# RWKV scan of a two-block network: two heads as full-array products, gram products of the heads in turn

## The chip, the cores and the metric

The kernel runs on one core of a Trainium2 chip. The metric is the device time of one execution in microseconds (us), the median of several runs. The engines are TensorE (PE in the rows, its weight loads PEld), VectorE (DVE), ScalarE (ACT), GpSimd (POOL) and SyncE (SP, which issues the DMAs here).

## What is computed

Two network blocks run one after the other on 256 latent and 256 context tokens of width 2048. The first holds sliding-window attention and latent attention, the second a mixer of pooling and RWKV-7 heads, and then an attention layer. The change lies in the RWKV part alone: 16 heads of width 64, two directions, and for each head a state of 64x64 that is updated token by token over 512 tokens:

```
def step(S, xs):
    r, w, k, v, a, b = xs
    sa = jnp.einsum('bhvk,bhk->bhv', S, a)
    S = S * w[:, :, None, :] + sa[..., None] * b[:, :, None, :] + v[..., None] * k[:, :, None, :]
    return S, jnp.einsum('bhvk,bhk->bhv', S, r)
```

The decay w and the gate a come out of low-rank products (`tanh(shift(wd)) @ w2`, `shift(ad) @ a2`), and the result of the scan is normalised over each head of each token.

## The kernel before

The scan is done in chunks: NCH = 8 chunks of L = 64 tokens. One unit of work, the generator `rwkv(b, d)`, takes two heads (block b of 128 feature rows, head 0 on partitions 0 to 63, head 1 on 64 to 127) and one direction d; there are 16 units. A unit makes the decays (L1156 to L1191), the scaled keys BK and queries AQ (L1197 to L1214), a bonus product `bon` (L1220), the gram products of keys and queries of each chunk (L1241) with masked evictions (L1244 to L1246), the transposed keys BKs (L1265) and values SV (L1274, L1279), and the inverse of a triangular matrix of each chunk (from 8 rows upwards, L1341 to L1366), which leaves TT.

Then comes the chain over the 8 chunks, one step for each. In a step five pairs of fp32 products, one product for each head, all write into one PSUM bank named `chain`: AQ's first part times SV (L1376), which VectorE copies to Rp (L1378); AQ's second part times SV (L1380); TT times Rp (L1388), copied into SV by VectorE and ScalarE (L1389, L1390); BKs times SV (L1393; not in the last step), added to the decayed state by VectorE (L1399, one instruction for each head); and QB times SV (L1404), which ScalarE evicts to y with its row sums (L1405). The next step starts from the state that L1399 wrote. The rows name a matmul's part of the array: 128\*64 and 64\*64 for the products of the chain, of which the two heads use two different column halves, 64\*128 for the gram products, 128\*128 for the whole array. An fp32 product leaves two records in the trace, a fp32r product one.

The units do not run alone. The loop over weight slices (`weights`, L327 on; products by `mm3`, L352 to L354) calls `fill` after each slice, and that moves every active unit on by one `yield`; up to four units are active, 12 yields apart. So TensorE's queue holds products `a` of the dense layers (fp32r, 128x512, three for each tile, with operands split into whi and wlo by L323 on ScalarE and L324 on VectorE) and among them the units' small products. The order of each engine's queue is fixed when the program is built, by a scheduler that lays out the instructions by the time that it takes them to need; at run time each engine goes through its queue in order and waits where an operand is not there.

Of the kernel before, what the change touches and what calls it, by code (L numbers as in the profile page):

```python
# [18 lines left out]
P = 128  # L19
# [4 lines left out]
L = 64  # L24
# [92 lines left out]
class Net:  # L117
# [933 lines left out]
    def ev_consts(self, ph):  # L1051
        nc, I = self.nc, self.I
        def load(n, shape):
            t = ph.tile(shape, F32, name="c_" + n)
            nc.sync.dma_start(out=t, in_=I[n])
            return t
        self.bones = load("bones", [P, P])
        self.bsel = load("bsel", [P, 2])
        self.smask = ph.tile([P, NT], F32, name="smask")
        nc.gpsimd.memset(self.smask, 1.0)  # L1060
        nc.gpsimd.memset(self.smask[:, 0:NT:L], 0.0)
        self.gmask = load("gmask", [P, P])
# [8 lines left out]
        nc.vector.tensor_scalar(self.kai, self.v("k_a", 0, 8), -0.5, 1.0, ALU.mult, ALU.add)  # L1071
        self.xscr = [self.pD.tile([1, BLK], F32, name=f"xscr{j}") for j in range(2)]
# [64 lines left out]

    def rwkv(self, ph, b, d, pads, lora, yscr, sums):
# [54 lines left out]
        AQ = ph.tile([P, 2, NCH, P], F32, tag="AQ", name=self.nm("AQ"), bufs=2)  # L1193
        BK = ph.tile([P, NCH, 2, L], F32, tag="BK", name=self.nm("BK"), bufs=BKB)
        for hh in range(2):
            r_ = half[hh]
            nc.vector.scalar_tensor_tensor(AQ[r_, hh, :, 0:L], ch(kkn)[r_], -1.0, Dp[r_, :, 0:L], ALU.mult, ALU.mult)  # L1197
# [14 lines left out]
        for hh in range(2):  # L1212
            r_ = half[hh]
            nc.vector.tensor_tensor(AQ[r_, hh, :, L:], ch(r)[r_], Dp[r_, :, 1:], op=ALU.mult)  # L1214
# [16 lines left out]

        NTr = ph.tile([P, NCH, L], F32, tag="NT", name=self.nm("NT"), bufs=NTB)
        QB = ph.tile([P, NCH, L], F32, tag="QB", name=self.nm("QB"), bufs=2)
        for hh in range(2):
            r_, o_ = half[hh], half[1 - hh]
            for c4 in range(0, NCH, 4):
                cs = slice(c4, c4 + 4)
                pb = self.bank("gram")
                for c in range(c4, c4 + 4):
                    lhs = BK[r_, c, :, :].rearrange("p a t -> p (a t)")  # L1240
                    mm(pb[:, (c - c4) * P : (c - c4 + 1) * P], lhs, AQ[r_, hh, c, :], start=True, stop=True)  # L1241
                pv = pb.rearrange("p (c t) -> p c t", c=4)
                mk = self.gmask.unsqueeze(1).broadcast_to([P, 4, P])
                nc.vector.tensor_tensor(NTr[r_, cs, :], pv[r_, :, 0:L], mk[r_, :, 0:L], op=ALU.mult)  # L1244
                nc.vector.tensor_tensor(QB[r_, cs, :], pv[r_, :, L:], mk[r_, :, L:], op=ALU.mult)
                nc.vector.tensor_tensor(AQ[o_, hh, cs, :], pv[o_], mk[o_], op=ALU.mult)  # L1246
            yield
# [11 lines left out]
        BKs = ph.tile([P, 2, NCH, L], F32, tag="BKs", name=self.nm("BKs"), bufs=2)  # L1259
        for hh in range(2):  # L1260
            r_ = half[hh]
            pb = self.bank("bkt")
            for c in range(NCH):
                src = BK[r_, c, :, :].rearrange("p a t -> p (a t)")
                nc.tensor.transpose(pb[:, c * L : (c + 1) * L], src, self.ident[r_, r_])  # L1265
            nc.scalar.copy(BKs[:, hh], ch(pb))
        yield
        SV = ph.tile([P, 2, NCH + 1, L], F32, tag="SV", name=self.nm("SV"), bufs=2)

        for c0 in (0, 1):  # L1270
            pb = self.bank("vt")
            for n in range(4 - c0):
                s = slice((2 * n + c0) * L, (2 * n + c0 + 2) * L)
                nc.tensor.transpose(pb[:, n * P : (n + 1) * P], v[:, s], self.ident)  # L1274
            if c0:
                for hh, c in ((1, NCH - 1), (0, 0)):
                    r_, o_ = half[hh], half[1 - hh]
                    o = 3 * P + hh * L
                    mm(pb[o_, o : o + L], v[r_, c * L : (c + 1) * L], self.ident[r_, r_], start=True, stop=True)  # L1279
# [34 lines left out]
        X2 = ph.tile([64, 16, 16], F32, tag="X2", name=self.nm("X2"))  # L1314
# [19 lines left out]
        TT = ph.tile([P, NCH, L], F32, tag="TT", name=self.nm("TT"), bufs=TTB)  # L1334
# [22 lines left out]
        nc.vector.tensor_tensor(TT, pairs(Z1, TT16), TT16, op=ALU.add)  # L1357
        yield
        pb = self.bank("x2")
        for c in range(NCH):  # L1360
            for q in (0, 64):
                mm(pb[q : q + 32, c * 32 : c * 32 + 32], Z2[q + 32 : q + 64, c, :], TT[q + 32 : q + 64, c, 32:64],
                   start=True, stop=True, tile_position=(q + 32, q))
        pv = pb[:, 0:256].rearrange("p (c t) -> p c t", c=NCH)
        nc.vector.tensor_copy(TT[0:32, :, 32:64], pv[0:32])
        nc.scalar.copy(TT[64:96, :, 32:64], pv[64:96])  # L1366

        y = ph.tile([P, NCH + 1, L], F32, tag="y", name=self.nm("y"), bufs=1)
# [3 lines left out]
        ps = self.bank("chain")  # L1372
        for c in range(NCH):
            last = c == NCH - 1
            for hh in range(2):
                mm(ps[half[hh], 0:64], AQ[:, hh, c, 0:L], SV[:, hh, c, :], start=True, stop=True)  # L1376
            Rp = ph.tile([P, L], F32, tag="Rp", name=self.nm("Rp"), bufs=2)
# [8 lines left out]
            for hh in range(2):  # L1386
                r_ = half[hh]
                mm(ps[r_, 64:128], TT[r_, c, :], Rp[r_], start=False, stop=True, skip_group_check=True)  # L1388
            nc.vector.tensor_copy(SV[half[0], 0, c, :], ps[half[0], 64:128])  # L1389
            nc.scalar.copy(SV[half[1], 1, c, :], ps[half[1], 64:128])  # L1390
            if not last:
                for hh in range(2):
                    mm(  # L1393
                        ps[half[hh], 128:192], BKs[:, hh, c, :], SV[:, hh, c, :],
                        start=False, stop=True, skip_group_check=True,
                    )
                for hh in range(2):
                    r_ = half[hh]
                    nc.vector.scalar_tensor_tensor(  # L1399
                        SV[r_, hh, c + 1, :], ps[r_, 128:192], DL[r_, c : c + 1], SD[r_], ALU.mult, ALU.add  # L1400
                    )
# [6 lines left out]
        y8 = y[:, 0:NCH]  # L1408
        wide = lambda t: t.unsqueeze(2).broadcast_to([P, NCH, L])
        nc.vector.tensor_scalar(mean, mean, 1.0 / L, None, ALU.mult)  # L1410
        nc.vector.tensor_tensor(y8, y8, wide(mean), op=ALU.subtract)
        sq = self.t512("sq").rearrange("p (c t) -> p c t", c=NCH)
        nc.scalar.activation(sq, y8, AF.Square)
# [6 lines left out]
        nc.vector.tensor_tensor(y8, y8, wide(rs), op=ALU.mult)  # L1420
        nc.scalar.copy(y[:, NCH], y[:, 0])
# [4 lines left out]
        for c0 in (0, 1):  # L1426
            pb = self.bank("yt")
            for n in range(4):
                src = y[:, 2 * n + c0 : 2 * n + c0 + 2, :].rearrange("p c t -> p (c t)")
# [570 lines left out]
```

## Time and profile before

| what | value |
|---|---|
| median of 3 runs | 3386.61 us (3378.92 to 3392.72) |
| profiled execution | 3385.91 us, span 3384.1 us |
| TensorE busy | 3198.0 us (95%), 21218 instructions |
| VectorE busy | 2051.4 us (61%) |
| ScalarE busy | 1541.6 us (46%) |
| GpSimd busy | 195.8 us (6%) |
| RWKV stretch | 1620 to 2640 us of the span |

A matmul's record lasts longer than TensorE is held by it, since matmuls are pipelined: what one costs is read from the time from its start to the start of the next one. "Busy" of TensorE can so be near 100% while the starts lie far apart.

### The profile page before, as it was taken

The page shows a single profiled execution, that of the slowest core. Times are in us where ns is not written, and L with a number is a line of the kernel's source. Part 1 is how long each engine was busy: PE and PEld are TensorE (multiplying, and loading weights), DVE is VectorE, ACT ScalarE, POOL GpSimd, SP SyncE. Part 2 cuts the span into 40 slices and gives each one's busy share as a digit, 9 for nine tenths or more (in the row PEclk, how much of TensorE's full clock was granted, in tenths as well). Part 3 has the DMA queues.
Part 4 walks back from the last instruction along what each step waited for, and adds up shares of the span by engine and source line. Part 5 has one row for each costly group of instructions (what it writes and reads, how often), then busy time and mean ns, then how long its engine had stood idle before and what let it go on. Part 6 is the DMA issues. An engine that isn't in the chain of part 4 may idle for free. (4 is left out here: it accounts for less than half of the span.)

```text
span 3384.1 us, 56050 instructions
## 1 busy us (share of the span) xinstructions
PE 3198.0 (95%) x21218; PEld 2384.4 (70%) x21218; DVE 2051.4 (61%) x4487; ACT 1541.6 (46%) x3461; POOL 195.8 (6%) x277
## 2 busy tenths in 40 slices
PE   5999999989989999898999989999999999899998
PEld 2567777767877777665766666666666678778887
DVE  2456455543476666442776676777777655867767
ACT  2424444442366655442344434444444433636654
POOL 0000000000001110000000000000000001200000
PEclk8999999999999999999999999999999999999999
DMA  7843444358654655988534222222323444544454
GB/s 299 307 161 126 144 140 144 131 198 292 213 166 155 212 193 194 369 340 320 170 119 125 76 76 79 73 73 66 99 80 93 133 168 131 174 129 144 132 174 157
DMA packets 270784, 556.27 MB, mean 164 GB/s; under 512 B 122928, under 2 KB 150704, under 8 KB 244912
## 3 DMA queue, kind: packets, MB, share of 16 engines
q1 hardware_dynamic: 270512, 552.68, 49.0%
q8 instruction: 167, 2.74, 0.3%
q14 instruction: 105, 0.86, 0.1%
HBM read 517.46 MB, written 35.13 MB: 163 GB/s over the span
## 5 line engine op out<-in xcount | busy, mean ns | idle before, releaser
L324 DVE TENSOR_TENSOR wlo<-raw,whi 128x512 fp32r<-128x512 f32 (+2 forms) x1000 | 658.7, 668 | 610.4 <-ACT whi L323 573.3
L352 PE MATMUL a<-hhi,whi 128*128 128x512 f32 (+1 forms) x2752 | 975.9, 357 | 32.6 <-ACT whi L323 29.6
L323 ACT CAST whi<-raw 128x512 fp32r<-128x512 f32 (+2 forms) x1000 | 591.8, 599 | 865.1 <-PE a L353 448.9
L353 PE MATMUL a<-hlo,whi 128*128 128x512 f32 (+1 forms) x2752 | 950.5, 347 | 0.2 <-DVE hlo L445 0.2
L354 PE MATMUL a<-hhi,wlo 128*128 128x512 f32 (+1 forms) x2752 | 938.6, 349 | 5.6 <-DVE wlo L324 5.1
L352 PEld LDWEIGHTS a<-hhi,whi 128*128 128x128 f32 x2752 | 524.3, 191 | 192.9 <-ACT whi L323 79.6
L354 PEld LDWEIGHTS a<-hhi,wlo 128*128 128x128 f32 x2752 | 518.5, 191 | 72.5 <-DVE wlo L324 14.1
L353 PEld LDWEIGHTS a<-hlo,whi 128*128 128x128 f32 x2752 | 525.3, 191 | 54.2 <-issue 3.0
L352 PE MATMUL a<-whi,hhi 128*128 128x512 f32 (+1 forms) x672 | 262.8, 401 | 16.1 <-ACT sq L613 5.9
L353 PE MATMUL a<-wlo,hhi 128*128 128x512 f32 (+1 forms) x672 | 264.5, 394 | 0.3
L456 POOL TENSOR_TENSOR rs<-st,mhalf 128x4 f32<-128x4 f32 (+3 forms) x109 | 140.9, 1293 | 2097.5 <-DVE st L453 1910.8
L354 PE MATMUL a<-whi,hlo 128*128 128x512 f32 (+1 forms) x672 | 260.4, 390 | 0.0
L260 PE MATMUL mv<-mraw,cs 128*32 128x512 f32 x1536 | 234.0, 632 | 21.4 <-DMA mraw<-mod_w 21.3
L352 PEld LDWEIGHTS a<-whi,hhi 128*128 128x128 f32 x672 | 127.1, 191 | 74.2 <-issue 22.2
L353 PEld LDWEIGHTS a<-wlo,hhi 128*128 128x128 f32 x672 | 128.9, 192 | 30.0 <-DVE wlo L324 5.4
L354 PEld LDWEIGHTS a<-whi,hlo 128*128 128x128 f32 x672 | 128.9, 192 | 26.0 <-issue 1.1
L565 ACT ACTIVATE pr<-sc,nm 128x512 f32<-128x512 f32 (+1 forms) x128 | 81.0, 632 | 93.3 <-DVE nm L562 62.6
L1385 ACT ACTIVATE SD<-SV,DL 64x64 f32<-64x64 f32 x224 | 77.2, 345 | 63.3 <-DVE SV L1399 60.1
L556 DVE TENSOR_REDUCE mx<-sc 128x1 f32<-128x512 f32 (+1 forms) x128 | 78.9, 617 | 40.3 <-PE sc L354 23.4
L1399 DVE SCALAR_TENSOR_TENSOR SV<-chain,DL,SD 64x64 f32<-64x64 f32 x224 | 63.3, 283 | 59.7 <-PE chain L1393 51.6
L572 ACT ACTIVATE pr<-pr,rc 128x512 f32<-128x512 f32 (+1 forms) x128 | 85.6, 669 | 22.0 <-DVE rc L571 21.9
L260 PEld LDWEIGHTS mv<-mraw,cs 128*32 128x32 f32 x1536 | 33.9, 110 | 85.1 <-issue 38.6
(371 smaller groups left out, 4465.9 us busy)
## 6 DMA issues: line engine op xcount, KB each, us to landing
mraw<-mod_w SPq DMA_DIRECT2D x192, 1024.0 KB, 5.0
raw<-od_in SPq DMA_DIRECT2D x88, 512.0 KB, 3.5
raw<-swa_in SPq DMA_DIRECT2D x72, 512.0 KB, 3.6
raw<-ev_rkv SPq DMA_DIRECT2D x64, 384.0 KB, 3.5
raw<-ev_in SPq DMA_DIRECT2D x48, 512.0 KB, 3.6
raw<-swa_out SPq DMA_DIRECT2D x40, 512.0 KB, 5.6
raw<-ev_out SPq DMA_DIRECT2D x40, 512.0 KB, 3.4
raw<-mla_g SPq DMA_DIRECT2D x64, 256.0 KB, 3.1
```

The lines of the kernel that those rows point to most:

```text
L260: nc.tensor.matmul(pb[32 * j : 32 * j + 32, :], cs[:, 32 * k + 30 - 2 * n : 32 * k + 62 - 2 * n], raw[:, j, :], start=(n == 0 and q == 0), ...
L323: nc.scalar.copy(whi, raw)
L324: nc.vector.tensor_tensor(wlo, raw, whi.bitcast(F32), op=ALU.subtract)
L352: mm(out, ah, bh, start=first, stop=False, skip_group_check=shared)
L353: mm(out, ah, bl, start=False, stop=False, skip_group_check=shared)
L354: mm(out, al, bh, start=False, stop=last, skip_group_check=shared)
L456: self.nc.gpsimd.tensor_tensor(dst, stv, mv, op=ALU.pow)
L556: nc.vector.reduce_max(mx, sc, axis=AX.X)
L565: nc.scalar.activation(pr[:, :n], sc, AF.Exp, scale=scale, bias=nm, accum_out=sm)
L572: nc.scalar.activation(pr[:, :n], pr[:, :n], AF.Copy, scale=rc)
L1385: nc.scalar.activation(SD[r_], SV[r_, hh, c, :], AF.Copy, scale=DL[r_, c : c + 1])
L1399: nc.vector.scalar_tensor_tensor(SV[r_, hh, c + 1, :], ps[r_, 128:192], DL[r_, c : c + 1], SD[r_], ALU.mult, ALU.add)
```

## The change

The products of the two heads become one product of the whole array. For that SV of both heads (128 rows, 2x64 columns) is the moving operand and AQ, BKs, QB and TT of both heads stand side by side as 128 stationary columns; the result is 128x128, of which only the two diagonal 64x64 blocks are used. For QB and TT, which reach over one head's rows only, the stationary tile has zeros beside them: they become tiles that are zeroed once (`ev_consts`), two for QB and one for TT. Since a diagonal block of each head has its own columns, the evictions to Rp (VectorE), to y (ScalarE) and to TT (VectorE) become two instructions each, of 64 partitions, where they were one of 128. The layout of AQ and BKs changes with it (chunk first, then part, then head).

The gram products take the two heads in turn, chunk by chunk, into two PSUM banks, where they took four chunks of one head and then of the next into one bank. The masked eviction of 64x512 becomes two of 64x256. The key transposes become 8 of 128x128 for a unit instead of 16 of one head's 64 rows. The last value transpose, that was two small products for the first and last chunk, becomes a transpose of a tile into which GpSimd copies those two chunks (`ends`); the same function replaces a ScalarE copy of y's first chunk. The second part of the low-rank products (wl, L1162) goes over all 128 rows instead of 64. X2 takes the memory of N16.

```
-        nc.vector.tensor_tensor(wl[hd], wa[hd], wh[hd].bitcast(F32), op=ALU.subtract)
+        nc.vector.tensor_tensor(wl, wa, wh.bitcast(F32), op=ALU.subtract)
-            mm(pb, wl[hd, j], tl[j][hd], start=False, stop=True)
+            mm(pb, wl[:, j], tl[j], start=False, stop=True)
...
+        for c4 in range(0, NCH, 4):
+            pbs = [self.bank("gram") for _ in range(2)]
+            for c in range(c4, c4 + 4):
+                for hh in range(2):
+                    mm(pbs[hh][:, (c - c4) * P : (c - c4 + 1) * P], lhs, AQ[r_, c, :, hh, :], start=True, stop=True)
+            for hh in range(2):
...
-                nc.vector.tensor_tensor(AQ[o_, hh, cs, :], pv[o_], mk[o_], op=ALU.mult)
+                for i in range(2):
+                    nc.vector.tensor_tensor(AQ[o_, cs, i, hh, :], pv[o_, :, s], mk[o_, :, s], op=ALU.mult)
...
-            for c in range(NCH):
-                nc.tensor.transpose(pb[:, c * L : (c + 1) * L], src, self.ident[r_, r_])
+            for c in range(c4, c4 + 4):
+                nc.tensor.transpose(
+                    pb[:, (c - c4) * P : (c - c4 + 1) * P], BK[:, c, :, :].rearrange("p a t -> p (a t)"), self.ident
+                )
...
-            for hh in range(2):
-                mm(ps[half[hh], 0:64], AQ[:, hh, c, 0:L], SV[:, hh, c, :], start=True, stop=True)
-            nc.vector.tensor_copy(Rp, ps[:, 0:64])
+            mm(ps[:, 0:P], heads(AQ[:, c, 0]), SV[:, :, c, :], start=True, stop=True)
+            for hh in range(2):
+                nc.vector.tensor_copy(Rp[half[hh]], blk(0, hh))
-            for hh in range(2):
-                mm(ps[half[hh], 192:256], AQ[:, hh, c, L:], SV[:, hh, c, :], start=False, stop=False, skip_group_check=True)
+            mm(ps[:, 3 * P :], heads(AQ[:, c, 1]), SV[:, :, c, :], start=False, stop=False, skip_group_check=True)
...
-                mm(ps[r_, 64:128], TT[r_, c, :], Rp[r_], start=False, stop=True, skip_group_check=True)
+            mm(ps[:, P : P + L], heads(TT[:, c]), Rp, start=False, stop=True, skip_group_check=True)
...
-                for hh in range(2):
-                    mm(
-                        ps[half[hh], 128:192], BKs[:, hh, c, :], SV[:, hh, c, :],
+                mm(
+                    ps[:, 2 * P : 3 * P], heads(BKs[:, c]), SV[:, :, c, :],
...
-                mm(ps[r_, 192:256], QB[r_, c, :], SV[r_, hh, c, :], start=False, stop=True, skip_group_check=True)
-            nc.scalar.activation(y[:, c, :], ps[:, 192:256], AF.Copy, accum_out=mean[:, c : c + 1])
+            mm(ps[:, 3 * P :], heads(QB[:, c]), SV[:, :, c, :], start=False, stop=True, skip_group_check=True)
+                nc.scalar.activation(y[r_, c, :], blk(3 * P, hh), AF.Copy, accum_out=mean[r_, c : c + 1])
```

## Rows read from the trace of the kernel before

**Rows 1.** Busy time by stretch: us, then busy us (instructions) of each engine, clock, DMA.

```profile
1620.00:1700.00 80.00, 79.98 (x574) 56.25 (x572) 64.45 (x126) 27.23 (x64) 4.21 (x11) 1.00 0.51 159
...
2200.00:2300.00 100.00, 97.08 (x879) 67.15 (x877) 76.57 (x168) 43.41 (x118) 6.75 (x14) 1.00 0.28 74
...
1620.00:2640.00 1020.00, 986.67 (x8096) 667.71 (x8094) 744.87 (x1683) 442.58 (x1185) 72.44 (x139) 0.98 0.33 94
```

**Rows 2.** TensorE's timeline within one chain step: start us, length us, instruction, count.

```profile
2316.55 0.40 PE L353 MATMUL a<-hlo,whi 128*128 128x512 f32 x1
2316.88 0.34 PE L1380 MATMUL chain<-SV,AQ 128*64 128x64 f32 x4
2317.14 0.33 PE L1388 MATMUL chain<-Rp,TT 64*64 64x64 f32 x4
2317.41 0.50 PE L354 MATMUL a<-hhi,wlo 128*128 128x512 f32 x1
2317.74 0.39 PE L352 MATMUL a<-hhi,whi 128*128 128x512 f32 x1
2317.97 0.40 PE L353 MATMUL a<-hlo,whi 128*128 128x512 f32 x1
2318.30 0.34 PE L1393 MATMUL chain<-SV,BKs 128*64 128x64 f32 x4
2318.56 0.50 PE L354 MATMUL a<-hhi,wlo 128*128 128x512 f32 x1
2318.89 0.40 PE L352 MATMUL a<-hhi,whi 128*128 128x512 f32 x1
```

**Rows 3.** TensorE's timeline where fp32 products use the whole array.

```profile
1809.52 0.39 PE L353 MATMUL a<-hlo,whi 128*128 128x512 f32 x1
1809.75 1.02 PE L1220 MATMUL bon<-r,c_bones 128*128 128x512 f32 x2
...
1810.85 0.40 PE L353 MATMUL a<-hlo,whi 128*128 128x512 f32 x1
...
2303.81 0.73 PE L464 MATMUL sums<-c_bsel,sq 128*128 128x2 f32 x6
```

**Rows 4.** TensorE's timeline around a low-rank product.

```profile
2304.98 0.47 PE L1161 MATMUL zw<-tl,wah 128*128 128x512 f32 x1
2305.38 0.49 PE L1162 MATMUL zw<-tl,wal 64*128 64x512 f32 x1
2305.80 0.28 PE L1380 MATMUL chain<-SV,AQ 128*64 128x64 f32 x2
```

**Rows 5.** TensorE's timeline: an inversion product of alternating heads, then gram products.

```profile
2273.35 1.15 PE L1341 MATMUL inv<-t,Z 64*64 64x64 f32 x32
...
2281.99 2.05 PE L1241 MATMUL gram<-AQ,BK 64*128 64x128 f32 x16
```

**Rows 6.** Groups by line in 1620 to 2640: count, busy us, mean ns, idle before.

```profile
L1246 DVE TENSOR_TENSOR AQ<-gram,c_gmask 64x512 f32<-64x512 f32 x64 | 44.1, 689 | 1.1
L1244 DVE TENSOR_TENSOR NT<-gram,c_gmask 64x256 f32<-64x256 f32 x64 | 26.9, 421 | 7.4 <-PE gram L1241 5.9
L1378 DVE COPY Rp<-chain 128x64 f32<-128x64 f32 x116 | 26.0, 224 | 85.6 <-PE chain L1376 71.4 <-ACT whi L323 9.5 <-ACT pu L1115 1.1
L1405 ACT ACTIVATE y<-chain 128x64 f32<-128x64 f32 x115 | 25.6, 223 | 48.9 <-PE chain L1404 46.7 <-DVE X L1303 0.3 <-ACT BKs L1266 0.3
L1405 ACT ACTIVATION_READ_ACCUMULATOR y<-chain 128x1 f32 x115 | 22.8, 198 | 0.7
L1292 POOL MEMSET X<- 64x272 f32 x15 | 4.8, 319 | 94.8 <-DMA xscr<-X 86.0 <-ACT Dp L1184 8.8
```

**Rows 7.** Waits of TensorE in 1620 to 2640: us in total, times, longest.

```profile
PE bon L1220 <- DVE r L1218: 17.1, 7, 5.4
```

**Rows 8.** TensorE's timeline: the first products of two successive chain steps.

```profile
2315.72 0.34 PE L1376 MATMUL chain<-SV,AQ 128*64 128x64 f32 x4
...
2320.85 0.34 PE L1376 MATMUL chain<-SV,AQ 128*64 128x64 f32 x4
```

More of the change, by code (lines that the diff above doesn't have):

```diff
@@ L1071, in ev_consts @@
         nc.vector.tensor_scalar(self.kai, self.v("k_a", 0, 8), -0.5, 1.0, ALU.mult, ALU.add)
+        self.qb2 = [ph.tile([P, NCH, 2, L], F32, name=f"qb{j}") for j in range(2)]
+        self.tt2 = ph.tile([P, NCH, 2, L], F32, name="tt")
+        for t in self.qb2 + [self.tt2]:
+            nc.gpsimd.memset(t, 0.0)
         self.xscr = [self.pD.tile([1, BLK], F32, name=f"xscr{j}") for j in range(2)]
@@ L1136, in pool_mean, with ends @@
                 nc.sync.dma_start(out=yscr[:, 2 * g + f, :], in_=o)
+    def ends(self, t):
+        w = self.t512("ends", cols=2 * L)
+        self.nc.gpsimd.tensor_copy(w.rearrange("p (c t) -> p c t", c=2), t[:, NCH - 1 :: 1 - NCH, :])
+        return w
     def rwkv(self, ph, b, d, pads, lora, yscr, sums):
@@ L1232, in rwkv @@
         NTr = ph.tile([P, NCH, L], F32, tag="NT", name=self.nm("NT"), bufs=NTB)
-        QB = ph.tile([P, NCH, L], F32, tag="QB", name=self.nm("QB"), bufs=2)
-        for hh in range(2):
[L1235 to L1239, printed above, removed]
+        QB = self.qb2[(2 * b + d) % 2]
+        mk = self.gmask.unsqueeze(1).broadcast_to([P, 4, P])
+        for c4 in range(0, NCH, 4):
+            cs = slice(c4, c4 + 4)
+            pbs = [self.bank("gram") for _ in range(2)]
+            for c in range(c4, c4 + 4):
+                for hh in range(2):
+                    r_ = half[hh]
                     lhs = BK[r_, c, :, :].rearrange("p a t -> p (a t)")
-                    mm(pb[:, (c - c4) * P : (c - c4 + 1) * P], lhs, AQ[r_, hh, c, :], start=True, stop=True)
-                pv = pb.rearrange("p (c t) -> p c t", c=4)
-                mk = self.gmask.unsqueeze(1).broadcast_to([P, 4, P])
+                    mm(pbs[hh][:, (c - c4) * P : (c - c4 + 1) * P], lhs, AQ[r_, c, :, hh, :], start=True, stop=True)
+            for hh in range(2):
+                r_, o_ = half[hh], half[1 - hh]
+                pv = pbs[hh].rearrange("p (c t) -> p c t", c=4)
                 nc.vector.tensor_tensor(NTr[r_, cs, :], pv[r_, :, 0:L], mk[r_, :, 0:L], op=ALU.mult)
-                nc.vector.tensor_tensor(QB[r_, cs, :], pv[r_, :, L:], mk[r_, :, L:], op=ALU.mult)
-                nc.vector.tensor_tensor(AQ[o_, hh, cs, :], pv[o_], mk[o_], op=ALU.mult)
+                nc.vector.tensor_tensor(QB[r_, cs, hh, :], pv[r_, :, L:], mk[r_, :, L:], op=ALU.mult)
+                for i in range(2):
+                    s = slice(i * L, i * L + L)
+                    nc.vector.tensor_tensor(AQ[o_, cs, i, hh, :], pv[o_, :, s], mk[o_, :, s], op=ALU.mult)
             yield
@@ L1257, in rwkv @@
         yield
-        BKs = ph.tile([P, 2, NCH, L], F32, tag="BKs", name=self.nm("BKs"), bufs=2)
-        for hh in range(2):
-            r_ = half[hh]
+        BKs = ph.tile([P, NCH, 2, L], F32, tag="BKs", name=self.nm("BKs"), bufs=2)
+        for c4 in range(0, NCH, 4):
             pb = self.bank("bkt")
-            for c in range(NCH):
-                src = BK[r_, c, :, :].rearrange("p a t -> p (a t)")
-                nc.tensor.transpose(pb[:, c * L : (c + 1) * L], src, self.ident[r_, r_])
-            nc.scalar.copy(BKs[:, hh], ch(pb))
+            for c in range(c4, c4 + 4):
+                nc.tensor.transpose(
+                    pb[:, (c - c4) * P : (c - c4 + 1) * P], BK[:, c, :, :].rearrange("p a t -> p (a t)"), self.ident
+                )
+            nc.scalar.copy(BKs[:, c4 : c4 + 4].rearrange("p c h k -> p (c h k)"), pb)
         yield
-        SV = ph.tile([P, 2, NCH + 1, L], F32, tag="SV", name=self.nm("SV"), bufs=2)
+        SV = ph.tile([P, 2, NCH, L], F32, tag="SV", name=self.nm("SV"), bufs=2)
+        vw = self.ends(ch(v))
         for c0 in (0, 1):
             pb = self.bank("vt")
[L1272 to L1279, printed above, removed]
+            for n in range(4):
+                src = v[:, (2 * n + c0) * L : (2 * n + c0 + 2) * L] if 2 * n + c0 < NCH - 1 else vw
+                nc.tensor.transpose(pb[:, n * P : (n + 1) * P], src, self.ident)
             pv = pb.rearrange("p (n t) -> p n t", n=4)
@@ L1356, in rwkv @@
         nc.scalar.copy(Z2[96:128], pv[96:128])
-        nc.vector.tensor_tensor(TT, pairs(Z1, TT16), TT16, op=ALU.add)
+        pz = pairs(Z1, TT16)
+        for hh in range(2):
+            r_ = half[hh]
+            nc.vector.tensor_tensor(TT[r_, :, hh, :], pz[r_], TT16[r_], op=ALU.add)
         yield
@@ L1372, in rwkv @@
         ps = self.bank("chain")
+        heads = lambda t: t.rearrange("p h t -> p (h t)")
+        blk = lambda o, hh: ps[half[hh], o + hh * L : o + hh * L + L]
         for c in range(NCH):
             last = c == NCH - 1
+            mm(ps[:, 0:P], heads(AQ[:, c, 0]), SV[:, :, c, :], start=True, stop=True)
+            Rp = ph.tile([P, L], F32, tag="Rp", name=self.nm("Rp"), bufs=2)
             for hh in range(2):
[L1376 to L1380 removed]
+                nc.vector.tensor_copy(Rp[half[hh]], blk(0, hh))
+            mm(ps[:, 3 * P :], heads(AQ[:, c, 1]), SV[:, :, c, :], start=False, stop=False, skip_group_check=True)
             if not last:
@@ L1385, in rwkv @@
                     nc.scalar.activation(SD[r_], SV[r_, hh, c, :], AF.Copy, scale=DL[r_, c : c + 1])
-            for hh in range(2):
-                r_ = half[hh]
-                mm(ps[r_, 64:128], TT[r_, c, :], Rp[r_], start=False, stop=True, skip_group_check=True)
-            nc.vector.tensor_copy(SV[half[0], 0, c, :], ps[half[0], 64:128])
-            nc.scalar.copy(SV[half[1], 1, c, :], ps[half[1], 64:128])
-            if not last:
-                for hh in range(2):
-                    mm(
-                        ps[half[hh], 128:192], BKs[:, hh, c, :], SV[:, hh, c, :],
-                        start=False, stop=True, skip_group_check=True,
-                    )
+            mm(ps[:, P : P + L], heads(TT[:, c]), Rp, start=False, stop=True, skip_group_check=True)
+            nc.vector.tensor_copy(SV[half[0], 0, c, :], ps[half[0], P : P + L])
+            nc.scalar.copy(SV[half[1], 1, c, :], ps[half[1], P : P + L])
+            if not last:
+                mm(
+                    ps[:, 2 * P : 3 * P], heads(BKs[:, c]), SV[:, :, c, :],
+                    start=False, stop=True, skip_group_check=True,
+                )
                 for hh in range(2):
@@ L1419, in rwkv @@
         yield
-        nc.vector.tensor_tensor(y8, y8, wide(rs), op=ALU.mult)
-        nc.scalar.copy(y[:, NCH], y[:, 0])
+        nc.vector.tensor_tensor(y, y, wide(rs), op=ALU.mult)
+        yw = self.ends(y)
         yield
@@ L1428, in rwkv @@
             for n in range(4):
-                src = y[:, 2 * n + c0 : 2 * n + c0 + 2, :].rearrange("p c t -> p (c t)")
+                c = 2 * n + c0
+                src = y[:, c : c + 2, :].rearrange("p c t -> p (c t)") if c < NCH - 1 else yw
                 nc.tensor.transpose(pb[:, n * P : (n + 1) * P], src, self.ident)
```

25 lines of the change are left out of this document (12 added, 13 removed).

## The prediction

> **What bounds the kernel now.** I read the page's engine sums first, then the busy time by stretch, since the change touches only the stretch from 1620 to 2640 us in which the RWKV units run. There TensorE is busy 986.7 of 1020 us, VectorE 744.9 and ScalarE 442.6 [rows 1]. Next I read TensorE's waits: the longest, for `bon`, comes to 17.1 us [rows 7], so TensorE almost never lacks an operand. But busy is not the same as well used, and so the third view is the timeline, start to start. Two dense products `a` that follow each other start 0.23 us apart (2317.74 to 2317.97). Where one chain product stands between them, three steps take 0.33, 0.26 and 0.33 us: 0.92 instead of 0.46 without it, so it costs 0.46 us. Where L1380 and L1388 stand together the steps are 0.33, 0.26, 0.27, 0.33, together 1.19: the pair costs 0.73 [rows 2]. The group's own steps are the 0.26; the rest, 0.10 before it and 0.10 in the `a` that comes two later, is paid for each time the queue leaves the whole array for parts of it and comes back.
>
> Is it the parts, or that the products are fp32? `bon` answers: it is fp32 on the whole array, starts 0.23 after the `a` ahead of it, and from its start to that of the second `a` behind it are 1.10 us, of which 0.23 is the first `a` [rows 3]. That is 0.87 for 512 columns, 0.22 for 128, with nothing at entry or exit. For few columns the weight loads could bind instead; six records (three products) of two columns take 0.73 us with their last one's full length [rows 3], so at most 0.24 a product. I take 0.22.
>
> **The change part by part.** The sum is against the profiled execution, 3385.9 us; its span is 3384.1, and the median of the three runs is 0.7 above it.
>
> *Chain.* There are 16 units x (7 x 5 + 4) = 624 groups. The whole timeline of the stretch shows them in 496 clusters; in about 400 both neighbours use the whole array, 292 of one group and 104 of the pair, and rows 2 show one of each. A single group falls from 0.46 to 0.22 and saves 0.24, 292 x 0.24 = 70 us; the pair falls from 0.73 to 0.44 and saves 0.29, 104 x 0.29 = 30. The other 124 groups stand beside gram or inversion products, which go on using parts; they save between 0.04 (0.26 - 0.22) and 0.24, and I take 0.1, 12 us. Chain: 112.
>
> *Low-rank.* Steps of 0.40 and 0.42 [rows 4] become two of 0.23: 0.36 x 32 products = 12 us.
>
> *Gram.* Eight products of one head take 2.05 us, 0.26 each [rows 5], 256 of them 66 us. No row shows 64\*128 products of alternating heads. The nearest is the inversion: sixteen products of 64 columns, heads in turn, take 1.15, 0.072 each, 0.144 for 128 columns [rows 5]. If the heads run side by side into two banks as they do there, 256 x (0.26 - 0.144) = 30 us are saved; if not, nothing. I take 30.
>
> *Key and value transposes.* Three visits to a part of the array in each unit, two for BK and one for the last value block, become whole-array ones; at the 0.24 of a single group, 16 x 3 x 0.24 = 12 us.
>
> TensorE loses 112 + 12 + 30 + 12 = 166 us of work, which would leave 854 of 1020.
>
> *What is added.* VectorE: a second Rp copy in each of 128 steps, 0.22 each [rows 6], 28 us; in each of 64 gram evictions two of 64x256 for one of 64x512, 2 x 0.42 - 0.69 = 0.15 [rows 6], 10 us; a second TT eviction, of the size of L1246's 0.69, 16 times, 11 us. That is 49, so 745 becomes 794. ScalarE: a second activation with its accumulator read, 0.22 + 0.20 [rows 6], 128 times, 54 us, 443 becomes 497. GpSimd: 32 copies of 128x128 that no row shows; a memset twice as wide is 0.32 [rows 6], and a copy might take from half of that to a microsecond. One stands before the value transposes, one before the last transposes. Behind them in GpSimd's queue are the units' memsets and the small powers for the norms; who waits is TensorE at the transposes and then ScalarE's evictions. GpSimd is busy 72 of 1020 us [rows 1] and other units' work covers one unit's wait, so I take 0; uncovered it is 32 x 1 = 32 us. The three first memsets, about a microsecond each, lie beside dense products. The wider wl, moved X2 and new layouts cost nothing: instruction count and row length stay.
>
> *Where the gain goes.* The chain's path grows by a copy (0.22 and some gap) and an eviction with its read (0.42), since they use the same bank one after the other and the next step's first product follows y's eviction. A step takes 5.13 us now [rows 8]; its products alone account for 0.46 + 0.73 + 0.46 + 0.46 = 2.1, which becomes 1.1. TensorE has to fill the growing wait with dense products further ahead, and their wlo comes from VectorE. VectorE would be needed 794 of 854 us, 93%. The most it does in a stretch now is 81% (64.5 of 80 us) [rows 1], and that it already comes late at times is what the waits for `bon` show: TensorE stood up to 5.4 us for its r [rows 7]. At 93% for VectorE the stretch is 854 long and the gain 166; at 77%, its share in the dense 2200 to 2300, it is 794 / 0.77 = 1031 and the gain is nothing. Neither end is shown, since VectorE's share now follows TensorE's pace. I take 86%, a little above the 81% it has reached: 794 / 0.86 = 923, a gain of about 97. I set it at 100, 60% of the work removed.
>
> **The rivals.** *All of it (B).* VectorE keeps up; 3386 - 166 = 3220. For it: VectorE's instructions on different tiles wait little in the chain stretches. Against: 93% has no row.
>
> *VectorE and the chain's own path take most (C).* VectorE at 78 to 82%, gain 17 to 51, about 3350. For it: the waits of [rows 7].
>
> *No change (D).* The two ends meet: 77% of VectorE, or GpSimd's copies queue behind its waiting memsets and eat what is left; 3386.
>
> *Slower (E).* The chain's path becomes the bound, as the units overlap only as far as single-buffered tiles (y, TT) allow: y of the next unit cannot be written before the last one's has been transposed. Then each step takes 5.13 + 0.25 + 0.42 = 5.8, 128 x 0.67 = 86 us more, 3472. It decides once a unit's eight steps and its tail of norm and transposes outlast the 854 / 16 = 53 us that TensorE needs for a unit; eight steps of 5.13 are 41 now, and of 5.8 are 46, with 7 us left for the tail. The steps hold dense products now, that can move out, which speaks against it.
>
> *Concurrency lost (F).* The heads' products lie side by side in column halves now, and the whole-array product sends both heads' 128 columns through in turn. If entering and leaving the parts were free, each of 624 groups would go from 0.11 for its four records (0.26 less the 0.15 to the next product) to 0.22: 69 us more, less gram's 30: 3425. Rows 2 against rows 3 speak against it, as the whole-array product carries no 0.10 at its edges. The Trainium skill, TensorEngine Tiling (Array Packing), section Overview, says the same in general: for a row or column dimension of at most 64 tiles give up to twice the speed; its Key Properties say that a change of mode drains TensorE, with no figure. This trace has the figure, and here the edges cost more than the halves give.
>
> **How the numbers follow.** The forecast (A), gain 60 to 140, 3246 to 3326, has 0.57; B and what lies near it, gain over 140, 0.17; C 0.12; D 0.06; E 0.06; F 0.02. Below 3210 and above 3368 I leave about 0.17, E, F, most of D and the tail of B. My own case reaches from 3246 to 3326, most likely 3386 - 100 = 3286. Half a per cent is 17 us, about what a measurement of this kernel can tell from no change: faster by more than that are A, B and C, 0.86; within it D, 0.06; slower E and F, 0.08.
>
> **What would show it.** Chain products in the rows as 128\*128, 128 columns, starting 0.23 after an `a`, with the next start about 0.22 on and no 0.33 behind; else D or F. Gram records in pairs that start almost together; if 0.11 apart, that 30 us is missing. L1161 to its second product 0.23. VectorE's share in 2200 to 2300 well above 77%; if it stays at 77 to 82%, C. TensorE's waits: `bon` and products that follow Rp, SV and y will grow; I expect some 60 to 70 us of new waiting in place of 17. A clock below full speed behind long waits would add to that. The forecast fails if GpSimd's copies show up as a long wait of the transposes, or if TensorE's waits for y lead, which is E.

## The result, and the profile after

The changed kernel takes 3403.7 us (median of 6 runs, 3399.4 to 3411.6) and the kernel before 3386.0 beside it. The ratio is 1.0059 with an interval of 1.0043 to 1.0074: 18 us slower, where 100 us less was forecast. The profiled execution of after took 3404.2 us with a span of 3402.3.

The busy time by stretch of after, to be held against [rows 1] (columns: stretch, its length, then busy us and instructions of PE, PEld, DVE, ACT, POOL, then granted clock, DMA share, GB/s):

```profile
1620.00:2640.00 1020.00, 921.30 (x6683) 675.22 (x6682) 768.69 (x1825) 479.09 (x1364) 86.11 (x167) 0.96 0.31 90
2200.00:2300.00 100.00, 89.41 (x732) 68.28 (x731) 77.79 (x180) 44.71 (x126) 9.90 (x18) 0.97 0.24 66
2500.00:2600.00 100.00, 83.37 (x593) 63.42 (x591) 73.98 (x186) 48.06 (x139) 5.32 (x9) 0.86 0.27 77
```

TensorE is busy 921 of 1020 us, 65 less than before, and VectorE 769. No engine is full, and yet the stretch has become longer. (The chains run on beyond this window: the last step starts at 2718 us before and at 2740 in after.) The waits of TensorE in the same stretch (us in total, times, longest), against [rows 7]:

```profile
PE bon L1231 <- DVE r L1229: 43.3, 10, 8.8
PE chain L1393 <- ACT y L1419: 27.6, 68, 1.6
PE z L1365 <- DVE T L1359: 4.2, 3, 1.7
PE chain L1397 <- DVE Rp L1396: 4.1, 10, 0.9
```

The wait for `bon` went from 17.1 to 43.3 us, and a new one stands second: the first product of a chain step (L1393) waits for the eviction of y (L1419). The timeline shows how (start us, length us, instruction, count, idle before it and its releaser; TensorE, VectorE and ScalarE together, dense products left out where they follow each other):

```profile
2034.89 0.49 PE L1393 MATMUL chain<-SV,AQ 128*128 128x128 f32 x2 [0.44 <-ACT y L1419]
2035.41 0.46 DVE L1396 COPY Rp<-chain 64x64 f32<-64x64 f32 x2 [0.74 <-PE chain L1393]
...
2036.15 0.38 PE L1397 MATMUL chain<-SV,AQ 128*128 128x128 f32 x2
...
2036.37 0.33 PE L1403 MATMUL chain<-Rp,tt 128*128 128x64 f32 x2
...
2036.96 0.22 DVE L1404 COPY SV<-chain 64x64 f32<-64x64 f32 x1
...
2037.27 0.21 ACT L1405 COPY SV<-chain 64x64 f32<-64x64 f32 x1 [0.20 <-DVE SV L1404]
...
2037.53 0.49 PE L1407 MATMUL chain<-SV,BKs 128*128 128x128 f32 x2
...
2038.30 0.59 DVE L1413 SCALAR_TENSOR_TENSOR SV<-chain,DL,SD 64x64 f32<-64x64 f32 x2
...
2039.25 0.38 PE L1416 MATMUL chain<-SV,qb 128*128 128x128 f32 x2
...
2039.67 0.22 ACT L1419 ACTIVATE y<-chain 64x64 f32<-64x64 f32 x1 [0.34 <-PE chain L1416]
2039.70 0.39 PE L353 MATMUL a<-hlo,whi 128*128 128x512 f32 x1
...
2039.89 0.20 ACT L1419 ACTIVATION_READ_ACCUMULATOR y<-chain 64x1 f32 x1
2039.94 0.40 PE L354 MATMUL a<-hhi,wlo 128*128 128x512 f32 x1
2040.11 0.22 ACT L1419 ACTIVATE y<-chain 64x64 f32<-64x64 f32 x1
2040.34 0.20 ACT L1419 ACTIVATION_READ_ACCUMULATOR y<-chain 64x1 f32 x1
2040.59 0.49 PE L1393 MATMUL chain<-SV,AQ 128*128 128x128 f32 x2 [0.26 <-ACT y L1419]
...
2041.16 0.39 PE L353 MATMUL a<-hlo,whi 128*128 128x512 f32 x1
```

From one first product to the next are 5.70 us, where [rows 8] have 5.13. Seventeen dense products stand in this step, so TensorE's own wait for y is only 0.26. But the last product of the step starts at 2039.25, the state has been ready since 2038.89, and the next step begins only when both activations and both reads of y are over, at 2040.54: they evict other columns of the bank that L1393 writes. That 1.3 us is path, nearly all of it filled with work that TensorE could have done at another time.

The groups of four of the instructions that the change doubles, in 1620 to 2640 of after, against [rows 6] (count, busy us, mean ns, idle before):

```profile
L1396 DVE COPY Rp<-chain 64x64 f32<-64x64 f32 x224 | 49.5, 221 | 100.9 <-PE chain L1393 98.8
L1419 ACT ACTIVATE y<-chain 64x64 f32<-64x64 f32 x224 | 48.8, 218 | 33.8 <-PE chain L1416 30.3
L1419 ACT ACTIVATION_READ_ACCUMULATOR y<-chain 64x1 f32 x224 | 44.4, 198 | 2.0
L1262 DVE TENSOR_TENSOR AQ<-gram,c_gmask 64x256 f32<-64x256 f32 x120 | 45.4, 418 | 1.0
```

An instruction over 64 partitions takes as long as one over 128 did (221 against 224 ns, 218 against 223), so two cost twice as much, as the prediction reckoned.

### The profile page after: what moved, and what is told of

Read it like the earlier page. It is cut to its first block, busy times and chain, and to the rows that moved or that the text cites. A ratio compares the mean times of both kernels' runs of the same rounds, so it can differ in the third digit from the quotient of the medians.

```text
span 3402.3 us, 53480 instructions
## 1 busy us (share of the span) xinstructions
PE 3145.9 (92%) x19794; PEld 2406.9 (71%) x19794; DVE 2097.7 (62%) x4695; ACT 1597.8 (47%) x3701; POOL 215.1 (6%) x312
## 5 line engine op out<-in xcount | busy, mean ns | idle before, releaser
L354 PEld LDWEIGHTS a<-hhi,wlo 128*128 128x128 f32 x2752 | 519.8, 192 | 63.4 <-DVE wlo L324 12.3
L1396 DVE COPY Rp<-chain 64x64 f32<-64x64 f32 x256 | 56.6, 221 | 111.8 <-PE chain L1393 109.3
L1393 PEld LDWEIGHTS chain<-SV,AQ 128*128 128x128 f32 x256 | 39.2, 189 | 78.7 <-ACT y L1419 74.4
```

What stands on the lines that cost most here:

```text
L354: mm(out, al, bh, start=False, stop=last, skip_group_check=shared)
L1396: nc.vector.tensor_copy(Rp[half[hh]], blk(0, hh))
```

## The experiments

The theory after the result (S where the expectations use a letter): **the serial path of a chain step**, from first product to first product, is the bound, and the two additional evictions lengthen it. The rivals: VectorE's work is the bound (V; 768.7 us plus what stands behind `bon`); or the waits come from where TensorE's queue has its products, whatever the evictions cost (P). Under the path theory a kernel with the same work but a shorter path is faster; under the VectorE theory only less work on VectorE helps. Each run changes the program, so the scheduler also lays out the order of its queues anew. All ratios are to the kernel before, with 95% intervals; L is 64 and P is 128 in the diffs.

**One eviction for both heads again.**

```
-            for hh in range(2):
-                nc.vector.tensor_copy(Rp[half[hh]], blk(0, hh))
+            nc.vector.tensor_copy(Rp, ps[:, 0:L])
...
-            for hh in range(2):
-                r_ = half[hh]
-                nc.scalar.activation(y[r_, c, :], blk(3 * P, hh), AF.Copy, accum_out=mean[r_, c : c + 1])
+            nc.scalar.activation(y[:, c, :], ps[:, 3 * P : 3 * P + L], AF.Copy, accum_out=mean[:, c : c + 1])
```

> The changed kernel (3404 us) with Rp and y evicted by one instruction of 128 partitions each, as before; head 1 of both then takes the wrong block, so this part of the result is left wrong and only the time is read. Theory S (the serial path of the chain and VectorE's queue between two chains set the period of a unit, and TensorE's saved work is only filler): a step loses a copy of 0.25 and an eviction with its read of 0.42 us, 128 steps x 0.67 = 86 us, so 3404 - 86 = about 3320. Theory V (VectorE's total work of 49 us more is what took the gain): 28 us of it go, about 3375. Theory P (the waits come from where the queue of TensorE has bon and the first chain product, whatever the evictions cost): about 3404.

Measured 3341.6 us, 0.9864 (0.9836 to 0.9893): 62 less than after and 44 less than before.

**Of these, only y in one instruction** (the second part of the diff above).

> The changed kernel with only y evicted by one instruction of 128 partitions (head 1's y is left wrong). Theory S: 128 x 0.42 = 54 us less, 3350. Theory V: VectorE's work is unchanged, so 3404. Theory P: 3404.

Measured 3377.6 us, 0.997 (0.9955 to 0.9986): 26 less than after. That leaves some 36 of the 62 for Rp, though y's two instructions are the longer ones. Why is not shown. In the trace of this kernel TensorE's clock is at the lower of its two levels (1.2 GHz) for 85 us between 1620 and 2640, and for 51 with one eviction each; in the steps that lie wholly at full clock the means are 6.33 us in after, 5.87 here and 5.75 with one eviction each, and by these y's part is the larger.

**The kernel before with two evictions.**

```
-            nc.vector.tensor_copy(Rp, ps[:, 0:64])
+            for hh in range(2):
+                nc.vector.tensor_copy(Rp[half[hh]], ps[half[hh], 0:64])
...
-            nc.scalar.activation(y[:, c, :], ps[:, 192:256], AF.Copy, accum_out=mean[:, c : c + 1])
+            for hh in range(2):
+                r_ = half[hh]
+                nc.scalar.activation(y[r_, c, :], ps[r_, 192:256], AF.Copy, accum_out=mean[r_, c : c + 1])
```

> The kernel before (3386 us) with its Rp copy and y eviction split into two instructions of 64 partitions, nothing else. Theory S: the chain's step grows by 0.67 us, 128 steps, up to 86 us more, 3440 to 3472; if half of it is still covered by TensorE's own longer groups, 3430. Theory V: 28 us of VectorE more beside a stretch of 1020 us in which it is busy 745: 3386 to 3414. If TensorE alone had bound the kernel before: 3386 to 3392.

Measured 3467.1 us, 1.0234 (1.0205 to 1.0264): 81 more than before. The two instructions and the read that each step gains last 0.22 + 0.42 = 0.64 us [rows 6], and 128 x 0.64 = 82, with VectorE and ScalarE far from full:

```profile
1620.00:2640.00 1020.00, 960.21 (x7460) 643.52 (x7460) 715.14 (x1657) 450.63 (x1297) 64.76 (x132) 0.93 0.30 85
```

That a longer path costs time is shown by this run more plainly than by any other. That the two sums agree is in part luck: the granted clock fell too, to 0.93 in this stretch from 0.98 in [rows 1] (more on this below).

**The products for y in a bank of their own**, in after:

```
-        ps = self.bank("chain")
+        ps, py = self.bank("chain"), self.bank("chainy")
...
-            mm(ps[:, 3 * P :], heads(AQ[:, c, 1]), SV[:, :, c, :], start=False, stop=False, skip_group_check=True)
+            mm(py[:, 0:P], heads(AQ[:, c, 1]), SV[:, :, c, :], start=True, stop=False, skip_group_check=True)
...
-            mm(ps[:, 3 * P :], heads(QB[:, c]), SV[:, :, c, :], start=False, stop=True, skip_group_check=True)
+            mm(py[:, 0:P], heads(QB[:, c]), SV[:, :, c, :], start=False, stop=True, skip_group_check=True)
...
-                nc.scalar.activation(y[r_, c, :], blk(3 * P, hh), AF.Copy, accum_out=mean[r_, c : c + 1])
+                nc.scalar.activation(y[r_, c, :], py[r_, hh * L : hh * L + L], AF.Copy, accum_out=mean[r_, c : c + 1])
```

> The changed kernel with the products for y (AQ's second part and QB) in a PSUM bank of their own, so that the next step's first product need not wait for y's two evictions. Theory S: 0.85 us of the path go, less what the following wait takes over, 60 to 100 us, 3304 to 3344; a second bank held for a whole chain may cost the other units some of it. Theory V and P: within 10 us of 3404.

> The kernel of the separate y bank (changed kernel, y's products in a bank of their own) once more, with more rounds, beside the two that follow: 3299, between 3292 and 3306.

Measured 3298.7 us, 0.9738 (0.9704 to 0.9771), and once more 3305.2 us, 0.9756 (0.9742 to 0.9771). Not one instruction is gone and no input is another; only the next step no longer waits for y (and the queues are laid out anew), and that takes about 100 us off: 128 x 2 x 0.42 = 107 of eviction left the path. This kernel computes the whole result and is 2.4% faster than the kernel before. The same stretch and waits of this kernel (columns as above):

```profile
1620.00:2640.00 1020.00, 973.19 (x7308) 738.26 (x7307) 840.94 (x2007) 533.60 (x1533) 96.86 (x172) 1.00 0.37 105
```

```profile
PE chain L1407 <- ACT SV L1405: 9.7, 26, 0.9
PE a L354 <- DVE wlo L324: 9.1, 6, 4.4
PE bon L1231 <- DVE r L1229: 6.4, 4, 3.4
```

VectorE runs at 840.9 of 1020 us, 82%, where it stood at 75% in after with the same instructions: so it was not what held after back. The wait for `bon` shrank from 43.3 to 6.4 by a change that does not touch `bon`, and the granted clock rose from 0.96 to 1.00.

**The same own bank in the kernel before** (py for L1380, L1404 and L1405).

> The kernel before with the products for y in a PSUM bank of their own, all else as before. Theory S alone: a step no longer waits for y's eviction and its read, 0.42 us and the wait behind it, 128 steps, 50 to 60 us, 3326 to 3336. Theory T (before, TensorE's queue and the path were tied, so that either alone moves the time little): TensorE has some 30 us of waits to give, 3356 to 3386. TensorE as the only bound: 3386.

Measured 3381.2 us, 0.9993 (0.9984 to 1.0003): nothing. A shorter path alone does not help the kernel before, whose TensorE is then busy 1000.6 of 1020 us. (The Trainium skill, Perfetto Trace Analysis, section Optimizing Tensor Performance, Matmuls, advises that independent groups of matmuls go to different PSUM banks, so that an eviction lies beside the next group's products. The own bank in after agrees with it by some 100 us; here the same move is worth nothing, since something else is as late.)

```profile
1620.00:2640.00 1020.00, 1000.64 (x8098) 685.88 (x8097) 745.70 (x1685) 434.74 (x1183) 77.10 (x138) 0.98 0.33 93
```

**Only TensorE's work smaller**, in the kernel before: the low-rank products over all rows and the key transposes of 128x128, whose evictions stay as many.

```
-            mm(pb, wl[hd, j], tl[j][hd], start=False, stop=True)
+            mm(pb, wl[:, j], tl[j], start=False, stop=True)
...
-                nc.tensor.transpose(pb[:, c * L : (c + 1) * L], src, self.ident[r_, r_])
+                nc.tensor.transpose(
+                    pb[:, (c - c4) * P : (c - c4 + 1) * P], BK[:, c, :, :].rearrange("p a t -> p (a t)"), self.ident
+                )
```

> The kernel before with the low-rank product over all rows and the key transposes as 128x128, nothing of the chain and no eviction changed: about 18 us of TensorE's work less (0.36 x 32 = 12, and 32 visits to a part of the array at up to 0.2 = 6), and no other engine's. TensorE as the bound: 3368. Theory S: the path of the chain is untouched, 3380 to 3386.

Measured 3392.6 us, 1.0019 (0.9997 to 1.0042): no gain either, where 18 us were possible. Its ten executions reach from 3374.9 us, at a mean granted clock of 0.980, to 3405.5 at 0.970, so a gain of a few us may be hidden by the clock. Together with the two runs before: in the kernel before, the path and TensorE's queue are tied. Longer on either side would cost, shorter on one side alone gives nothing.

**Less VectorE work**, in after: the subtraction of the token shift left out.

```
-        nc.vector.tensor_tensor(df.rearrange("p (s t) -> p s t", s=2), nb, u, op=ALU.subtract)
+        if n < P:
+            nc.vector.tensor_tensor(df.rearrange("p (s t) -> p s t", s=2), nb, u, op=ALU.subtract)
+            nb = df.rearrange("p (s t) -> p s t", s=2)
```

> The changed kernel without the subtraction in the token shift of k, r and v (the shifted values are so left wrong): 48 VectorE instructions of 0.69 us less, 33 us, all of them between the chain steps' own work. If VectorE's queue sets the stretch between the chains of two units (22.5 us), it falls to about 20.5 and the kernel to about 3371. If that stretch is set by something else (TensorE's order, the DMAs of the inverse), about 3404.

Measured 3388.4 us, 1.0009 (0.9996 to 1.0023): 15 less than after for some 33 us less of VectorE's work. The mean gap between the chains of two units falls from 22.5 to 21.7 us, the steps stay. VectorE's work counts for part of its time, in these gaps, and cannot explain a hundred.

**Gram products one head after the other**, in after (`for hh` outside `for c`).

> The changed kernel with the gram products again one head after the other within each four chunks, into the same two banks. In the trace of the changed kernel the heads' gram records start 0.11 us apart, as one head's did before, so the order should gain nothing: 3404 by theories S and V. If heads in turn do save the 30 us that I forecast and these are hidden, 3404 to 3434.

Measured 3419.1 us, 1.0097 (1.0071 to 1.0122): 15 more than after, with about 10 of uncertainty by the two intervals. The expectation misread the trace: of 256 pairs of gram records that could start together, 122 start within 0.05 us of each other in after, none in before. In this run 51 still do, so it took away a part of the alternation and not all of it.

**On top of the own bank: one copy to Rp; one activation for y; and y's row sums by one reduction on VectorE instead of 16 reads a unit.** The first two are the parts of the first experiment (y from `py[:, 0:L]`), the third is

```
-                nc.scalar.activation(y[r_, c, :], py[r_, hh * L : hh * L + L], AF.Copy, accum_out=mean[r_, c : c + 1])
+                nc.scalar.activation(y[r_, c, :], py[r_, hh * L : hh * L + L], AF.Copy)
...
+        nc.vector.reduce_sum(mean, y, axis=AX.X)
```

> The separate y bank with Rp copied by one instruction of 128 partitions (head 1's Rp is left wrong): the one extra eviction that still lies on the path of a step. If the path still sets the period: 128 x 0.25 = 32 us less, 3267. If TensorE and the path are tied again, as they were before the change: 3290 to 3299.

> The separate y bank with y evicted by one instruction (head 1's y is left wrong). By theory S this eviction is off the path now, so what was worth 26 us in the changed kernel is worth nothing here: 3294 to 3304. If instead ScalarE's total work counted, 54 us of 530 in the stretch, it would give about the same 26 us again: 3273.

> The separate y bank, with the row sums of y taken by one VectorE reduction of 128x512 for a unit instead of by the 16 accumulator reads on ScalarE (the result is the full one). ScalarE loses 256 x 0.20 = 51 us of work, VectorE gains 16 x 0.69 = 11 in the stretch between two chains. If ScalarE's queue is what the second eviction of y still costs (19 us for 54 of work), about 18 less and up to 11 more: 3287 to 3298. If only the path counts, which this doesn't touch: 3303 to 3316.

Measured 3291.6 us (0.9721, 0.9704 to 0.9738), 3286.0 us (0.9703, 0.9687 to 0.9719) and 3300.8 us (0.974, 0.9724 to 0.9756). Against the 3305.2 of the own bank that is 14, 19 and 4 less, the last within the intervals. One Rp copy takes 128 x 0.22 = 28 us off the path and gives half of it, so the path may again be close to tied with something else. That a single activation for y gives 19 although y is no longer on the path was not expected under S. It points to ScalarE's queue, but taking the accumulator reads from that, with a reduction on VectorE in their place, gave nothing that can be told from none. What sets the pace of this faster kernel stays open.

## Why the prediction was wrong

Two tables hold the argument. First, both forms of the products with both forms of the evictions, then with y in either bank (us; with y in its own bank each form has the evictions it came with, and for the whole array it is the mean of the two measurements):

| products | one eviction each | two each | y in its own bank |
|---|---|---|---|
| column halves | 3386 (before) | 3467 | 3381 |
| whole array | 3342 | 3404 (after) | 3302 |

The second row holds the rest of the change too (gram order, transposes, low-rank products, the split evictions of AQ and TT). Down each column this whole saves 44, 63 and 79 us; along the rows the second evictions of Rp and y cost 81 and 62. The change is the step down and the step to the right, 81 - 63 = 18 us. Second, the starts of the chain's first products, read one by one (us; a unit has seven intervals between its eight steps, and fifteen gaps lie between the last step of one unit and the first of the next), and the dense products `a` between them:

| kernel | mean of the 112 intervals | mean of the 15 gaps | `a` in an interval | `a` in a gap | first to last |
|---|---|---|---|---|---|
| before | 6.06 | 23.4 | 12.0 | 42.8 | 1029 |
| after | 6.43 | 22.5 | 13.0 | 35.9 | 1057 |
| one eviction each | 5.84 | 22.5 | 12.3 | 40.2 | 992 |
| before, two evictions | 6.86 | 23.0 | 13.5 | 32.1 | 1114 |
| own bank | 5.27 | 23.8 | 10.7 | 51.5 | 947 |
| before, own bank | 5.78 | 25.3 | 10.6 | 52.5 | 1027 |

The units' chains follow one another, so 112 intervals and 15 gaps make up the stretch: 112 x 6.43 + 15 x 22.5 = 1058, the 1057 of the table but for rounding. The first five differ in the interval and hardly in the gap. The last row shows the tie: with its own bank the kernel before has shorter steps (112 x 0.28 = 31 us less) and gaps that hold ten dense products more (15 x 1.9 = 29 us more). What left the steps came back in the gaps.

**The step that failed** is the first: "so TensorE almost never lacks an operand", and with it the bound. The short waits of [rows 7] were right as rows and wrong as a reading. The scheduler lays dense products between any two products of the chain, and more of them where the path is longer (table), so a long path shows as dense products in between and not as waiting. What the runs showed in its place is a path of the chain that is tied with TensorE's queue: made longer alone it cost 81 us, made shorter alone in the kernel before it gave nothing (0.9993), and without y's evictions in it the changed kernel gained 100. The sum gave this path no term. It bounded the gain by VectorE at 86%; VectorE stood at 75% in after and at 82% with the own bank, so that was not the bound.

**Rival E came nearest**, and got 0.06. Its mechanism (steps that lengthen by one copy and one eviction with its read) is what the second evictions did. It was set aside because a unit's steps and tail seemed to fit into TensorE's 53 us. With seven intervals of the 5.13 us of [rows 8] that leaves 17 us for the gap, and the measured gap is 23: 7 x 5.13 + 23.4 = 59, over the rival's own condition. Its 3472 stands too high because it leaves out what the rest of the change saves. What spoke against it, that dense products can move out of the steps, went the other way: 13.0 in an interval against 12.0, and 36 in a gap against 43, so they lack at `bon`. For the same reason its sign, waits for y in the lead, did not show: `bon` leads.

**The clock and the order of the queue** stand between the path and the time, and no run separates them. TensorE's clock is at its lower level for 31 us of 1620 to 2640 in before, 75 in after, 140 in the kernel before with two evictions and 7 with the own bank. The steps that lie wholly at full clock (106 to 112 of the 112) last 6.06, 6.33, 6.52 and 5.27 us in these four: the ranking is the same, but the second evictions then lengthen a step of the kernel before by 0.46 (112 x 0.46 = 52 of the 81 us). After's own six executions reach from 3399.4 us at a mean clock of 0.974 to 3411.6 at 0.970; at that slope the step from before's 0.979 to after's 0.973 is worth some 18 us, an estimate as large as the whole loss. The low stretches stand mostly around the waits for `bon`, so they probably follow from the longer path. As to the order: the same program profiled twice (own bank) has the same number of dense products in all 127 stretches between first products, while after and own bank agree in 10. No run held the order and changed the path alone, so differences of 4 to 26 us between two of these kernels may be order as well as cause.

**VectorE's share** was no bound. The prediction's own mark for rival C, 77 to 82% in 2200 to 2300, is met in after (77.8), and yet the own bank ran the same instructions at 85.3 there (80.7 in its second profile; over 1620 to 2640 both have 82%):

```profile
2200.00:2300.00 100.00, 95.32 (x791) 75.57 (x792) 85.28 (x197) 50.01 (x143) 9.79 (x21) 1.00 0.30 80
```

A share is a quotient, and it falls when the path stretches the time.

**The wait for `bon`** grew to 43.3 us for a reason that the prediction half named. Between two chains of after VectorE works through what has piled up (VectorE and TensorE, 2081.98 on):

```profile
2081.98 1.39 DVE L1225 TENSOR_TENSOR AQ<-r,Dp 64x512 f32<-64x512 f32 x2
...
2083.40 0.69 DVE L1433 TENSOR_TENSOR y<-y,rs 128x512 f32<-128x512 f32 x1
...
2084.57 1.39 DVE L1373 TENSOR_TENSOR tt<-inv,t 64x512 f32<-64x512 f32 x2
...
2086.58 0.74 DVE L1229 SCALAR_TENSOR_TENSOR r<-r,vec,k 128x512 f32<-128x512 f32 x1
...
2087.47 2.05 PE L1231 MATMUL bon<-r,c_bones 128*128 128x512 f32 x2 [5.64 <-DVE r L1229]
2087.91 1.02 DVE L324 TENSOR_TENSOR wlo<-raw,whi 128x384 fp32r<-128x384 f32 x2
```

TensorE stands 5.64 us, and the wlo of the next dense products comes behind that, at 2087.91. The clock falls with the wait, as the prediction said it might: it is at the lower level from 2084.9 to 2091.8, and `bon` lasts 2.05 us where [rows 3] have 1.02. In 2500 to 2600 the granted clock of after is 0.86, against 0.91 before and 1.00 with the own bank.

**Chain products** were sized right only where the operand was ready. L1416 at 2039.25 and the second start behind it at 2039.70 are 0.45 apart, less 0.23 for one dense product 0.22, as taken from [rows 3]. But L1393, L1397 and L1407 mostly wait for an eviction, and then their record is 0.49 long: from 2040.59 to 2041.16 are 0.57, less 0.23 that is 0.34. Both weight loads then stand behind the wait, where those of L1416 start 0.23 us ahead of it (PEld, after):

```profile
2039.02 0.42 PEld L1416 LDWEIGHTS chain<-SV,qb 128*128 128x128 f32 x2
2040.59 0.30 PEld L1393 LDWEIGHTS chain<-SV,AQ 128*128 128x128 f32 x2 [0.69 <-ACT y L1419]
```

The 112 us of the chain, where 0.22 was used for all, were too large by up to 0.12 for each of these. With the own bank 79 us, about half of the 166 that were reckoned for TensorE, showed as time; how much of the rest is mis-sized and how much hidden was not measured.

**Gram** gave about 15 of 30 us. After's timeline, TensorE:

```profile
2024.37 1.39 PE L1254 MATMUL gram<-AQ,BK 64*128 64x128 f32 x16
...
2026.42 1.16 PE L1254 MATMUL gram<-AQ,BK 64*128 64x128 f32 x8
...
2028.63 1.16 PE L1254 MATMUL gram<-AQ,BK 64*128 64x128 f32 x8
```

In the first four chunks the records start in pairs, 16 in 1.39 us; in the next four they do not, 8 in 1.16 each, as in one head's products before. The price was nearly right where they pair (0.17 a product against 0.144 taken and 0.26 before), but only 122 of 256 pairs got it: the order that the program got was not the one of the loop. Why is not shown.

**Nearly right** were the low-rank products, which here take 0.32 and 0.23 to their successors' starts, where [rows 4] have 0.40 and 0.42 and twice 0.23 was forecast:

```profile
2044.60 0.48 PE L1172 MATMUL zw<-tl,wah 128*128 128x512 f32 x1
2044.92 0.39 PE L1173 MATMUL zw<-tl,wal 128*128 128x512 f32 x1
2045.15 0.38 PE L1416 MATMUL chain<-SV,qb 128*128 128x128 f32 x2
```

GpSimd's copies also lay within their bounds (548 and 484 ns by the groups of L1146, between 0.16 and 1 us) and made no wait of the transposes in the trace.

## What to carry to other kernels

A queue with filler in it hides a serial path: before TensorE is called the bound, read the recurrence's steps from start to start over many of them, gaps included, and try the tie with the queue by lengthening the path (one eviction split in two). Compare the granted clock beside the times. A change that saves work on one of two tied chains and lengthens the other can lose, so both have to be shortened together: here whole-array products and a bank of its own for the output that nobody in the step needs. Two evictions of half the partitions took twice the time of one over all, and in this program an eviction stood on the path of the product that wrote the same bank next.

## What the runs showed of the hardware

- An instruction of VectorE or ScalarE over 64 partitions takes as long as one over 128: 221 and 218 ns against 224 and 223.
- Gram products of row halves run side by side where the records start in pairs: 16 records then took 1.39 us, and 8 took 1.16 where they did not.
- An fp32 whole-array product that has waited for its operand costs 0.34 instead of 0.22 us; its two weight loads start after the wait (2040.59) and not ahead of it (2039.02 for a product at 2039.25).
- TensorE's clock falls with a wait: after stands 5.64 us for `bon`, and from 2084.9 to 2091.8 the granted level is the lower one. The time of one program goes with it: 3374.9 us at a mean clock of 0.980, 3405.5 at 0.970 (kernel before with less TensorE work).
- A product waits for the eviction of other columns of its bank, as the program guards it: L1393 for y, 27.6 us in after, and no more with the own bank. The Trainium skill, PSUM — Partial Sum Buffer, section PSUM bank collisions raise a hardware error, asks for such a guard for each bank and quadrant of partitions and not for each address; the program's wait agrees with that, and no run here leaves it out. The page allows different quadrants at the same time, and the program is stricter: ScalarE's copy for one head (2037.27) waits 0.20 us for VectorE's copy for the other (2036.96), which reads other partitions of the bank. Whether the bank or the tile SV, which both write, is the reason is not shown, and what it would give to let them run together was not tried.
